# Expert units of a mixture-of-experts block: TensorE's instructions in the order of the program, transposes alternating with the combination, and three more pages for the mixer's weights

## The chip, the core and the metric

The kernel runs on one core of a Trainium2 chip. A core has a matrix engine (TensorE, PE in the profile), a vector engine (VectorE, DVE), an engine for activations (ScalarE, ACT), GpSimd (POOL), and SyncE (SP), which here issues the loads. Matmuls write PSUM banks of 512 floats a partition; the other engines read these. The metric is the device time of one launch in microseconds, the median of several.

## The reference

A decoder block over T = 512 tokens of width 1024, one layer, all in float32: a mixer (a Mamba-2 state-space branch and a gated short convolution on one input projection), then a mixture of experts. The expert part is what the change is about:

```python
scores = sigmoid(hf @ router_w); biased = scores + router_bias
...                                # the best 4 of 8 groups, in them the best 8 of 64 experts
gate = scores[e_idx] / sum * 2.5
...                                # tokens sorted by expert, in blocks
yb = (silu(xb @ w_gate[e]) * (xb @ w_up[e])) @ w_down[e]
routed = segment_sum(yb * row_gate[:, None], row_tok)
```

`w_gate` and `w_up` are 1024 x 256 for each of the 64 experts, `w_down` 256 x 1024: 3 x 64 matrices of 1 MB, 201 MB that are read once. Which tokens an expert gets is known only at run time.

## The kernel before

**Stages.** 0 to 540 us: the modulation (`w_ada`), the layer norm, the input projection and the mixer. 540 to 903: the mixer's output projections, the shared expert, the router and the ranking of the experts by their number of tokens. 903 to 943: the first gathers. 943 to 1605: the routed experts. 1605 to 1640: what is beyond the planned capacities, and the last norm.

**Expert units.** After the ranking, every rank has a fixed capacity in tokens (320, 192, 160, 128, 96, 64, 32). Ranks are packed into blocks of 128 token rows, and blocks into 32 units, whose kinds stand in a string (`ORDER`, one letter a unit): one expert of 128 rows; two experts at 64; four at 32; 96 + 32; and units of a full block and a packed one (three blocks in one unit). There are 41 blocks. A block's tokens are gathered from DRAM by an indirect DMA (L1075, GpSimd), whose indices come from matmuls with one-hot tiles (L1067), reductions (L1070) and an integer tile (L1072); `need_s` starts this. `xsplit`, called by `need_x`, turns the gathered rows with eight transposes (L141) and copies them out of PSUM into `xt` (L878, ScalarE).

**A unit's work** is the generator `ffn` (L905 is the matmul in `tiled`). Four quarters of the contraction come first, two k-steps of 128 each, for gate and up weights together (512 columns). A *full* block (one expert) has a float32 product made of three matmuls of split operands (`matmul3`, L144 to L146; the high part `wh` comes from ScalarE, L149, the low part `wl` from VectorE, L151). A *packed* block is done by `tiled`: one matmul for each expert, each in its own column strip of the array (`tile_position`), so that a k-step is two strips of 64 or four of 32 columns, which work beside each other. In the trace such a float32 matmul is two records. 336 k-steps of this kind are in the units. Behind the fourth quarter `act_t` makes the gate (Silu L886 on ScalarE, product L887 on VectorE), transposes it (L141) and copies it into `wkr` (L896 or a split). After a `yield` come the down matmuls (again `tiled` or `matmul3`, into `ps_y`), and `done` scales a block's output by the gate (L1108, VectorE) and splits it; a one-hot tile `oht` (L1104, GpSimd) says which token each row belongs to.

**Combination.** When two blocks are done, `combine()` adds them to the residual: for 4 token tiles and 2 halves, four matmuls `oht` x output (L1131 and L1132, full array, high and low part) into one of the two `ps_y` banks, and an addition on VectorE (L1137).

**What sets the order.** The steps of neighbouring units are interleaved in the program (quarters 1 to 3 of a unit, quarter 0 of the next, down matmuls of the first). Then a scheduler orders the instructions of every engine by priority and readiness in its own model; it may set any ready instruction between the strips of a k-step. Weight pieces of 1 MB are issued by SyncE, eight pieces ahead (`AHEAD`), into seven page pairs (`pair`, 1 MB, or two pages of 512 KB by `page`) and two more pages. In the mixer every 512 KB weight load (`load_cols`, L174; `ya_load`, L607) takes one of the fourteen pages of that ring. `beyond()` (L1307 to L1329) computes from the counts whether any tokens are left over.

Of the kernel before, what the change touches and what calls it, by code (L numbers as in the profile page):

```python
# [25 lines left out]
NPAIR = 7  # L26
NPAGB = 5
NPAPB = 2
STAT = ((0, 1),)
NST = sum(len(u) for u in STAT)  # L30

CAPS = ((1, 320), (4, 192), (3, 160), (4, 128), (16, 96), (13, 64), (21, 32)) + tuple((len(u), 128 // len(u)) for u in STAT)
GRP = 2
XA = 3
NXG = 3


# [2 lines left out]
NDEF = 2  # L40
FORD = "q0 r0 s0 q1 r1 s1 q2 r2 s2 q3 r3 s3"
NADA = 3
BEY = 100
ENG3 = ("PP", "VV", "VV", "VV")
NWK = 5
AD = "VVVV"
# [15 lines left out]
def block_kernel(ctx: ExitStack, tc: tile.TileContext, a, out, dbg=None):  # L62
# [40 lines left out]
    def page(shape, dt=F32, pool=None):  # L103

        n = 1
        for q in shape:
            n *= q
        assert n == 1024
        if pool:
            return pool.tile([P, *shape], dt, name="pg", tag="pg")  # L110
        assert dt == F32
        if not halves:
            halves.extend(reversed(two([1024])))
        h = halves.pop()
        return h.rearrange("p (a b) -> p a b", a=shape[0]) if len(shape) == 2 else h

    def wk():
        return wkp.tile([P, T], F32, name="wk")

# [50 lines left out]

    def load_cols(w, c0):

        v = page([KD, P])
        SY.dma_start(v, w[:, c0:c0 + P].rearrange("(k p) n -> p k n", p=P))  # L174
        return v

# [426 lines left out]

    def ya_load(qt, j):
        def f():
            v = page([4, 256])
            SY.dma_start(v, a["w_ssd_out"][0, qt * 512:(qt + 1) * 512, j * P:j * P + 256]  # L607
                         .rearrange("(k p) n -> p k n", p=P))
            return v
        plan(("ya", qt, j), f)  # L610
# [112 lines left out]
    for n, _ in enumerate(core):  # L723
        next(sc_g)
        for it in late:
            next(it, None)
    work_cm.__exit__(None, None, None)
    rt = ctx.enter_context(tc.tile_pool(name="rt", bufs=1))
    pb_ = ctx.enter_context(tc.tile_pool(name="pageb", bufs=NPAGB))
    ada4, ada8 = ada_rows(4), ada_rows(8)  # L730
# [132 lines left out]
            SY.dma_start(r, wd.rearrange("(p k) n -> p k n", k=2))  # L863
        return r

    def xsplit(src_ap, dst=None, whole=False):

        hi, lo = dst or [None if whole and i else hold.tile([P, KD, P], F32 if whole else FR, name="xt", tag="hm", bufs=8)
                         for i in range(2)]
        sv = src_ap.rearrange("p (d k) -> p k d", k=KD)  # L870
        for q in range(2):
            tp = bank("tr", 2)
            for k in range(4):
                transpose(tp[:, k * P:(k + 1) * P], sv[:, 4 * q + k, :])
            tv = tp.rearrange("p (k n) -> p k n", k=4)
            sl_ = slice(4 * q, 4 * q + 4)
            if whole:
                S.activation(hi[:, sl_, :], tv, AF.Copy)  # L878
            else:
                split_to(hi[:, sl_, :], lo[:, sl_, :], tv)  # L880
        return hi, lo

    def act_t(o, whole):

        sg = rt.tile([P, FE], F32, name="sg", bufs=2)
        S.activation(sg, o[:, :FE], AF.Silu)  # L886
        V.tensor_tensor(sg, sg, o[:, FE:], op=OP.mult)  # L887
        tp = bank("tr", 2)
        av = sg.rearrange("p (f j) -> p j f", j=2)
        for j in range(2):  # L890
            transpose(tp[:, j * P:(j + 1) * P], av[:, j, :])
        aw = wkp.tile([P, 4, P], F32 if whole else FR, name="wkr", tag="wk")
        ah, al = aw[:, 0:2], aw[:, 2:4]
# [14 lines left out]
    def ffn(blocks, xs, w, done, gp=False):  # L908


        es = sorted({e for b in blocks for e in b})
        split_e = sorted({b[0] for b in blocks if len(b) == 1})
        os_ = [bank(*(("pj", 3) if i < 3 else ("y", 2))) for i in range(len(xs))]
        for q in range(4):
            if q % 2 == 0:
                us = {e: w(e, q // 2) for e in es}
            uq = {e: us[e][:, :, q % 2 * 2:q % 2 * 2 + 2, :] for e in es}
            hl_ = {e: split(uq[e], GP if gp else None) for e in split_e}
            for o, (xh, xl), b in zip(os_, xs, blocks):
                for k in (2 * q, 2 * q + 1):  # L920
                    if len(b) == 1:
                        wh, wl = hl_[b[0]]
                        matmul3(o, xh[:, k, :], xl[:, k, :], wh[:, :, k % 2, :], wl[:, :, k % 2, :], k == 0, k == KD - 1)
                    else:
                        tiled(o, xh[:, k, :], [uq[e][:, :, k % 2, :] for e in b], k == 0, k == KD - 1)
            if q == 3:
                acts = [act_t(o, len(b) > 1) for o, b in zip(os_, blocks)]
            yield
        us = {e: w(e, 2) for e in es}
        wdn = {e: [split(us[e][:, j], GP if gp else None) for j in range(2)] for e in split_e}  # L930
        for i, ((ah, al), b) in enumerate(zip(acts, blocks)):
# [158 lines left out]
    def expert(blocks, sl_, xs, w):  # L1090
# [3 lines left out]
        def done(b, n, o):  # L1094
# [17 lines left out]
                S.activation(rt.tile([P, 1], F32, name="warm"), rw(yh)[:, 0:1], AF.Sqrt, bias=epsc, scale=0.0)  # L1112
            if n == 1:
                parts.append(res_[b])
                if len(parts) == GRP and not tail[0]:
                    combine()

        return ffn(blocks, xs, w, done)

    parts = []  # L1120
    rsum = rt.tile([P, NT, 2], F32, name="rsum")

    def combine(last=False):

        for t in range(NT):
            for n in range(2):
                ns_ = slice(n * 512, (n + 1) * 512)
                o = bank("y", 2)
                for i, (oht, yh, yl) in enumerate(parts):
                    oh_ = oht[:, t * P:(t + 1) * P]  # L1130
                    PE.matmul(o, oh_, yh[:, ns_], start=(i == 0), stop=False)  # L1131
                    PE.matmul(o, oh_, yl[:, ns_], start=False, stop=(i == len(parts) - 1))  # L1132
# [154 lines left out]
        while len(sl) < min(n, len(allb)):  # L1287
            sl.append(allb[len(sl)][1]())

    def need_x(n):  # L1290
        while len(xs) < min(n, len(allb)):
            i = len(xs)
            need_s(i + 1)
            xs.append(xsplit(sl[i][0], None, len(allb[i][0]) > 1))
            need_s(i + NXG)

    iota_t = rt.tile([P, T], F32, name="iota_t", tag="pt")
    GP.iota(iota_t, pattern=[[1, T]], base=0, channel_multiplier=0, allow_small_or_imprecise_dtypes=True)
    def beyond():
# [33 lines left out]
    running, i1 = {}, 0  # L1333
    for i, (u, j) in enumerate(steps):
        if j == 0:
            i0 = ublk[id(u)]
            i1 = i0 + len(u[1])
            need_x(i1)
            running[id(u)] = expert([b for b, _ in u[1]], sl[i0:i1], xs[i0:i1],
                                    lambda e, q, n=unum[id(u)]: take((n, e, q), AHEAD))  # L1340
        if i + XA < len(steps) and steps[i + XA][1] == 0 and len(xs) == i1:
            need_x(i1 + 1)
        if i == BEY:
            ostart, oend, obase, nov = beyond()
        tail[0] = i == len(steps) - 1
        next(running[id(u)], None)
    combine(True)


    ocur = rt.tile([P, 1], F32, name="ocur")  # L1350
# [98 lines left out]
```

## Time and profile before

| | |
|---|---|
| median of 3 runs | 1646.18 us |
| lowest, highest | 1641.13, 1926.16 us |
| profiled execution | 1641.05 us, of it 1639.3 us from the first to the last instruction |
| TensorE busy in the span | 1550.5 us (95%), mean granted clock 0.98 |
| VectorE, ScalarE, GpSimd busy | 988.3, 643.7, 305.0 us |
| DMA | 335.66 MB, mean 205 GB/s |

The records of matmuls overlap: the end of one is modelled and lies behind the start of the next. So a busy share near 100% says that TensorE was never without work, not that each matmul took its recorded time; what a matmul costs is read from its start to the next one's start.

### The profile page before, as it was taken

How to read it: one execution, taken by the hardware profiler on the slowest of the kernel's cores; microseconds unless marked ns; L12 is line 12 of the kernel's file. 1: busy time of each engine (PE TensorE's matmuls, PEld its weight loads, DVE VectorE, ACT ScalarE, POOL GpSimd, SP SyncE). 2: the span in 40 equal slices, each digit the busy share in tenths (PEclk: the TensorE clock that was granted, in tenths of full speed). 3: DMA queues.
4: the chain of work that ended last, by engine and by line, in shares of the span. 5: the costliest groups of instructions: out<-in, count | busy, mean ns of one | idle time of the engine just before them, and what ended most of it. 6: DMA issues, size and time to landing. Idle time of an engine off the chain costs nothing.

```text
span 1639.3 us, 22871 instructions
## 1 busy us (share of the span) xinstructions
PE 1550.5 (95%) x8253; PEld 1011.6 (62%) x8253; DVE 988.3 (60%) x1760; ACT 643.7 (39%) x926; POOL 305.0 (19%) x314
## 2 busy tenths in 40 slices
PE   6999999999999989899988899999999999999996
PEld 3687777777777867688766354554454444446533
DVE  5557778668848757445796363654455455457546
ACT  3556576545634445433552222232222223223323
POOL 0011110111001446500024211111111221112111
PEclk9999999999999989999988999999999999999998
DMA  9654332633450467535553779786978696799771
GB/s 275 170 151 107 82 87 65 153 85 87 116 125 1 155 200 230 164 88 167 199 174 103 253 288 364 273 314 231 369 287 301 249 402 238 280 381 351 277 287 61
DMA packets 193783, 335.66 MB, mean 205 GB/s; under 512 B 13348, under 2 KB 136580, under 8 KB 185348
## 3 DMA queue, kind: packets, MB, share of 16 engines
q1 hardware_dynamic: 182580, 303.73, 54.9%
q0 software_dynamic: 11088, 30.45, 6.8%
q8 instruction: 66, 1.08, 0.3%
q14 instruction: 49, 0.40, 0.1%
HBM read 334.58 MB, written 4.28 MB: 207 GB/s over the span
## 4 chain that ended last, share of the span: by engine, by line
PE 54%; DVE 6%; DMA 5%; POOL 2%; issue 2%; ACT 2%; SPq 0%; ACTq 0%; DVEq 0%; POOLq 0%
PE ps_pj L905 13%; PE ps_y L905 7%; PE ps_pj L144 6%; PE ps_pj L145 5%; PE ps_pj L146 5%; PE ps_y L1131 5%; PE ps_y L1132 5%; PE ps_tr L141 3%; DMA pr<-in_w_ada_dram 3%; POOL pg L357 2%; PE ps_y L144 1%; DVE wl L151 1%; DMA pr<-in_w_up_dram 1%; PE ps_y L145 1%; PE ps_y L146 1%
## 5 line engine op out<-in xcount | busy, mean ns | idle before, releaser
L151 DVE TENSOR_TENSOR wl<-pr,wh 128x1024 fp32r<-128x1024 f32 (+1 forms) x201 | 256.2, 1285 | 153.9 <-ACT wh L149 150.9
L144 PE MATMUL ps_pj<-hm,wh 128*128 128x512 f32 x680 | 276.6, 408 | 9.2 <-ACT wh L149 7.9
L149 ACT ACTIVATE wh<-pr 128x1024 fp32r<-128x1024 f32 (+1 forms) x207 | 201.1, 987 | 192.8 <-PE ps_pj L145 87.9
L146 PE MATMUL ps_pj<-hm,wl 128*128 128x512 f32 x680 | 269.2, 397 | 5.2 <-DVE wl L151 5.2
L145 PE MATMUL ps_pj<-hm,wh 128*128 128x512 f32 x680 | 268.4, 395 | 0.0
L905 PE MATMUL ps_pj<-pr,xt 128*32 128x512 f32 (+1 forms) x1472 | 252.1, 601 | 0.0
L144 PEld LDWEIGHTS ps_pj<-hm,wh 128*128 128x128 f32 x680 | 129.3, 190 | 43.7 <-ACT wh L149 9.9
L146 PEld LDWEIGHTS ps_pj<-hm,wl 128*128 128x128 f32 x680 | 129.1, 190 | 37.0 <-DVE wl L151 8.9
L145 PEld LDWEIGHTS ps_pj<-hm,wh 128*128 128x128 f32 x680 | 129.3, 190 | 29.5 <-issue 3.6
L1108 DVE SCALAR_TENSOR_TENSOR wk<-ps_y,red,pg 128x512 f32<-128x512 f32 x82 | 61.0, 749 | 118.8 <-PE ps_y L905 92.8
L1137 DVE TENSOR_TENSOR res<-res,ps_y 128x512 f32<-128x512 f32 x152 | 103.3, 687 | 47.5 <-PE ps_y L1132 47.0
L905 PEld LDWEIGHTS ps_pj<-pr,xt 128*32 128x32 f32 (+1 forms) x1472 | 58.2, 115 | 119.3 <-issue 114.0
L905 PE MATMUL ps_y<-pr,wkr 128*32 128x512 f32 (+1 forms) x736 | 117.5, 597 | 0.0
L1075 POOL DMA_INDIRECT pg<-h_d,idx x41 | 44.2, 1078 | 349.5 <-PE ps_tr L141 103.8
L1104 POOL TENSOR_SCALAR oht<-iota_t,tok 128x512 fp32r<-128x512 f32 x41 | 70.3, 1721 | 156.2 <-PE ps_y L1132 156.0
L886 ACT ACTIVATE sg<-ps_pj 128x256 f32<-128x256 f32 x44 | 16.9, 384 | 198.0 <-PE ps_pj L905 126.8
L357 POOL TENSOR_TENSOR pg<-pg,pr 128x1024 f32<-128x1024 f32 x28 | 75.3, 2706 | 68.7 <-ACT pr L355 68.6
L144 PE MATMUL ps_pj<-pr,wh 128*128 128x512 f32 x192 | 76.3, 398 | 10.1 <-ACT zs L422 10.1
L145 PE MATMUL ps_pj<-pr,wh 128*128 128x512 f32 x192 | 75.7, 394 | 0.0
L146 PE MATMUL ps_pj<-pr,wl 128*128 128x512 f32 x192 | 75.7, 394 | 0.0
L887 DVE TENSOR_TENSOR sg<-sg,ps_pj 128x256 f32<-128x256 f32 x44 | 18.5, 419 | 90.6 <-ACT sg L886 90.6
L407 DVE SCALAR_TENSOR_TENSOR wk<-ps_pj,cw,wk 128x511 f32<-128x511 f32 (+2 forms) x93 | 68.5, 743 | 7.6 <-ACT wk L405 7.3
(388 smaller groups left out, 2610.3 us busy)
## 6 DMA issues: line engine op xcount, KB each, us to landing
pr<-in_w_gate_dram SPq DMA_DIRECT2D x128, 512.0 KB, 8.3
pr<-in_w_up_dram SPq DMA_DIRECT2D x128, 512.0 KB, 9.0
pr<-in_w_down_dram SPq DMA_DIRECT2D x64, 1024.0 KB, 8.4
pr<-in_w_in_dram SPq DMA_DIRECT2D x88, 512.0 KB, 6.2
pr<-in_w_ada_dram SPq DMA_DIRECT2D x48, 512.0 KB, 5.1
bc<-acs_d POOLq DMA_DIRECT2D x32, 256.0 KB, 5.2
pr<-in_w_ssd_out_dram SPq DMA_DIRECT2D x16, 512.0 KB, 6.6
pr<-in_w_sc_out_dram SPq DMA_DIRECT2D x8, 512.0 KB, 4.8
```

Of the source, the lines that this page charges most:

```text
L144: PE.matmul(o, lh, rh, start=start, stop=False)
L145: PE.matmul(o, lh, rl, start=False, stop=False)
L146: PE.matmul(o, ll, rh, start=False, stop=stop)
L149: S.activation(hi, src, AF.Copy)
L151: V.tensor_tensor(lo, src, rw(hi), op=OP.subtract)
L357: GP.tensor_tensor(part[i], part[i], w, op=OP.add)
L407: V.scalar_tensor_tensor(acc[:, s:], o[:, :T - s], cw[:, 3 - s, tl:tl + 1], acc[:, s:], op0=OP.mult, op1=OP.add)
L905: PE.matmul(o[w * i:w * i + w, :], x[:, w * i:w * i + w], m, start=start, stop=stop, tile_position=(0, w * i))
L1104: GP.tensor_scalar(res_[b][0], iota_t, tok, None, op0=OP.is_equal)
L1131: PE.matmul(o, oh_, yh[:, ns_], start=(i == 0), stop=False)
L1132: PE.matmul(o, oh_, yl[:, ns_], start=False, stop=(i == len(parts) - 1))
L1137: V.tensor_tensor(ra[t][:, ns_], ra[t][:, ns_], o, op=OP.add)
```

## The change

It has two parts.

*The expert units.* `xsplit` and `combine` become generators, `xsteps` and `csteps`; the former yields after four transposes, the latter after the four matmuls and the addition of a bank. `act_t` is cut in two: `act_in` (Silu and product), and `act_t` (transposes), with a `yield` before and one behind it. A new `unit(n)` writes the order out: quarters 1 to 3 of unit n, quarter 0 of unit n+1 (`begin`), the transposes of n's activations, then the token transposes of unit n+2 alternating with a combination if two blocks are done (or the ring of outputs would be full), then n's down matmuls. In odd quarters the blocks of a unit come in reverse. From the third unit on this stands in `tc.manual_schedule(engines={PE})`: TensorE's instructions keep the order of the program, while the other engines are ordered by the scheduler as before. `beyond()` moves from the 100th step of the old list to just ahead of the unit with number 25.

*The mixer's loads.* `wpage` hands out, in turn, one of three new pages `sp` of the working pool and a page of the old ring, until the working pool is closed ahead of the experts.

```diff
+NSTR = 3
-XA = 3
+NRING = 3
+MAN = 2
-BEY = 100
+BEY = 25
...
+    def wpage(shape):
+
+        strm[0] += 1
+        if strm[0] % 2 and strm[0] > 0:
+            return work.tile([P, *shape], F32, name="sp", tag="sp", bufs=NSTR)
+        return page(shape)
...
     def load_cols(w, c0):
 
-        v = page([KD, P])
+        v = wpage([KD, P])
...
     def ya_load(qt, j):
         def f():
-            v = page([4, 256])
+            v = wpage([4, 256])
...
     work_cm.__exit__(None, None, None)
+    strm[0] = -1 << 30
...
-    def xsplit(src_ap, dst=None, whole=False):
+    def xsteps(src_ap, dst=None, whole=False):
...
+        def steps():
+            for q in range(2):
+                tp = bank("tr", 2)
+                for k in range(4):
+                    transpose(tp[:, k * P:(k + 1) * P], sv[:, 4 * q + k, :])
...
+                yield
+
+        return (hi, lo), steps()
...
-    def act_t(o, whole):
+    def act_in(o):
 
         sg = rt.tile([P, FE], F32, name="sg", bufs=2)
         S.activation(sg, o[:, :FE], AF.Silu)
         V.tensor_tensor(sg, sg, o[:, FE:], op=OP.mult)
+        return sg
+
+    def act_t(sg, whole):
+
         tp = bank("tr", 2)
...
-            for o, (xh, xl), b in zip(os_, xs, blocks):
+            for o, (xh, xl), b in list(zip(os_, xs, blocks))[::-1 if q % 2 else 1]:
...
             if q == 3:
-                acts = [act_t(o, len(b) > 1) for o, b in zip(os_, blocks)]
+                sgs = [act_in(o) for o in os_]
             yield
+        acts = [act_t(sg, len(b) > 1) for sg, b in zip(sgs, blocks)]
+        yield
...
                 parts.append(res_[b])
-                if len(parts) == GRP and not tail[0]:
-                    combine()
...
-    def combine(last=False):
-
+    def csteps(last=False):
+
+        ps_ = list(parts)
+        parts.clear()
         for t in range(NT):
             for n in range(2):
...
                     V.tensor_tensor(ra[t][:, ns_], ra[t][:, ns_], o, op=OP.add)
-        parts.clear()
+                yield
...
+    def begin(n):
+
+        u = units[n]
+        i0 = ublk[id(u)]
+        i1 = i0 + len(u[1])
+        need_x(i1)
+        running.append(expert([b for b, _ in u[1]], sl[i0:i1], xs[i0:i1], lambda e, q: take((n, e, q), AHEAD)))
+        next(running[n])
+
+    def unit(n):
...
+        u, last = units[n], n + 1 == len(units)
+        for _ in range(3):
+            next(running[n])
+        if not last:
+            begin(n + 1)
+        next(running[n])
+        xg_ = xs_steps(ublk[id(units[n + 2])] + len(units[n + 2][1])) if n + 2 < len(units) else iter(())
+        if len(parts) >= GRP or len(parts) + len(u[1]) > NRING or last and parts:
+            zipper(xg_, csteps())
+        else:
+            drain(xg_)
+        tail[0] = last
+        next(running[n], None)
...
+    with tc.manual_schedule(engines={mybir.EngineType.PE}):
+        for n in range(MAN, len(units)):
+            if n == BEY:
+                ostart, oend, obase, nov = beyond()
+            unit(n)
+        combine(True)
```

TensorE, in the second half of the units, a unit of four 32-column strips, before. One row of the order is one matmul instruction (two records in the trace); `ps_pj` is the gate and up product, `ps_y` a down product or a combination, `ps_st` the index matmul.

```order
L1067 MATMUL ps_st<-pay,oh 128x6
L905 MATMUL ps_pj<-pr,xt 32x512
L1131 MATMUL ps_y<-hm_70,oht 128x512
L1132 MATMUL ps_y<-hm_71,oht 128x512
L1131 MATMUL ps_y<-pr,oht 128x512
L1132 MATMUL ps_y<-pr,oht 128x512
...
L905 MATMUL ps_pj<-pr,xt 32x512 x28
L141 MATMUL ps_tr<-ident,sg 128x128 x2
L905 MATMUL ps_pj<-pr,xt 32x512 x3
L141 MATMUL ps_tr<-ident,pg 128x128 x4
L905 MATMUL ps_y<-pr,wkr 32x512 x16
```

The first strip of a k-step stands ahead of twenty combination matmuls, the other three behind them. The same engine after, a unit of that kind at the turn from one unit to the next:

```order
L931 MATMUL ps_pj<-pr,xt 32x512 x8
L152 MATMUL ps_tr<-ident,sg 128x128 x2
L152 MATMUL ps_tr<-ident,pg 128x128 x4
L1160 MATMUL ps_y<-pr,oht 128x512
L1161 MATMUL ps_y<-pr,oht 128x512
L1160 MATMUL ps_y<-rww,oht 128x512
L1161 MATMUL ps_y<-pg,oht 128x512
L152 MATMUL ps_tr<-ident,pg 128x128 x4
...
L931 MATMUL ps_y<-pr,wkr 32x512 x16
```

Quarter 0 of the next unit (x8) is whole, then come the gate's two transposes, then four token transposes and four combination matmuls in turn. In the order of the whole expert part, 77 of the 336 packed k-steps are cut by other instructions before, and 10 after, all of these in the first two units; TensorE changes from packed to full-array matmuls 130 times before and 65 times after.

ScalarE, after, at a turn from a unit to one with a full expert; `wh` is the high part of a weight piece, `sg` the Silu of the gate.

```order
L892 ACTIVATE xt<-ps_tr 128x512 x2
L160 ACTIVATE wh_80<-pr 128x1024
L160 ACTIVATE wh_76<-pr 128x1024
L160 ACTIVATE rww<-wk 128x512 x2
L160 ACTIVATE wh_78<-pr 128x1024
L160 ACTIVATE wh_80<-pr 128x1024
L908 ACTIVATE sg<-ps_pj 128x256
```

Two weight splits stand directly ahead of a Silu; ScalarE was ordered in this manner before as well.

SyncE, after, the first loads:

```order
L185 DMA sp<-in_w_ada_dram 128x8x128
L185 DMA pr<-in_w_ada_dram 128x8x128
L185 DMA sp<-in_w_ada_dram 128x8x128
L185 DMA pr<-in_w_ada_dram 128x8x128
L242 DMA wdt<-in_w_in_dram 128x8x32
L185 DMA sp<-in_w_in_dram 128x8x128
L185 DMA pr<-in_w_in_dram 128x8x128
```

Before, the same loads all went to `pr`; now every second one takes one of the three `sp` pages, in the same order.

## Rows read from the trace of the kernel before

**Rows 1.** Busy time by stage: stretch, length, engines, granted clock, DMA share, GB/s.

```profile
core 0: us, PE busy (x) PEld busy (x) DVE busy (x) ACT busy (x) POOL busy (x), PEclk, DMA share, GB/s
0.00:540.00 540.00, 507.90 (x2638) 395.27 (x2639) 374.20 (x720) 286.61 (x381) 57.91 (x120) 0.99 0.47 116
...
943.00:1605.00 662.00, 653.58 (x3804) 324.33 (x3803) 349.72 (x579) 182.21 (x293) 111.20 (x109) 1.00 0.82 303
```

**Rows 2.** Waits of TensorE, 943 to 1605: total us, times, longest.

```profile
PE ps_pj L145 <- DVE wl L151: 2.5, 3, 0.9
PE ps_pj L144 <- ACT wh L149: 1.7, 2, 1.6
```

**Rows 3.** TensorE's timeline, 1286 to 1312: start, busy us, instructions.

```profile
1292.89 1.05 PE L905 MATMUL ps_pj<-pr,xt 128*32 128x512 f32 x2
1293.87 0.50 PE L1131 MATMUL ps_y<-hm,oht 128*128 128x512 f32 x1
1294.20 0.39 PE L1132 MATMUL ps_y<-hm,oht 128*128 128x512 f32 x1
1294.43 0.39 PE L1131 MATMUL ps_y<-pr,oht 128*128 128x512 f32 x1
...
1298.61 0.40 PE L1132 MATMUL ps_y<-pr,oht 128*128 128x512 f32 x1
1298.93 6.21 PE L905 MATMUL ps_pj<-pr,xt 128*32 128x512 f32 x56
...
1307.32 3.64 PE L905 MATMUL ps_y<-pr,wkr 128*32 128x512 f32 x32
1310.90 0.71 PE L141 MATMUL ps_tr<-ident,pg 128*128 128x128 f32 x4
```

**Rows 4.** Groups of TensorE's instructions, 943 to 1605: busy us, mean ns, idle before.

```profile
L905 PE MATMUL ps_pj<-pr,xt 128*32 128x512 f32 (+1 forms) x1360 | 231.0, 599 | 0.0
L905 PE MATMUL ps_y<-pr,wkr 128*32 128x512 f32 (+1 forms) x656 | 106.6, 597 | 0.0
```

**Rows 5.** Costliest groups of the page, whole span, same columns.

```profile
L151 DVE TENSOR_TENSOR wl<-pr,wh 128x1024 fp32r<-128x1024 f32 (+1 forms) x201 | 256.2, 1285 | 153.9 <-ACT wh L149 150.9
...
L149 ACT ACTIVATE wh<-pr 128x1024 fp32r<-128x1024 f32 (+1 forms) x207 | 201.1, 987 | 192.8 <-PE ps_pj L145 87.9
...
L1137 DVE TENSOR_TENSOR res<-res,ps_y 128x512 f32<-128x512 f32 x152 | 103.3, 687 | 47.5 <-PE ps_y L1132 47.0
...
L886 ACT ACTIVATE sg<-ps_pj 128x256 f32<-128x256 f32 x44 | 16.9, 384 | 198.0 <-PE ps_pj L905 126.8
...
L887 DVE TENSOR_TENSOR sg<-sg,ps_pj 128x256 f32<-128x256 f32 x44 | 18.5, 419 | 90.6 <-ACT sg L886 90.6
```

**Rows 6.** Groups of VectorE's instructions in `beyond()`, 1380 to 1390.

```profile
L1309 DVE TENSOR_TENSOR key<-ps_st,caprow 128x64 f32<-128x64 f32 x1 | 0.2, 224 | 4.2 <-PE ps_st L1307 4.2
...
L1313 DVE SCALAR_TENSOR_TENSOR rem<-key,rem 128x64 f32<-128x64 f32 x3 | 0.7, 226 | 0.1
```

**Rows 7.** Busy time in slices of 41 us of the expert stretch.

```profile
984.00:1025.00 41.00, 37.52 (x221) 17.64 (x213) 14.56 (x32) 9.95 (x16) 6.67 (x8) 1.00 0.96 366
...
1107.00:1148.00 41.00, 40.93 (x175) 19.59 (x176) 19.16 (x30) 9.89 (x17) 7.83 (x9) 1.00 0.63 233
...
1476.00:1517.00 41.00, 40.86 (x237) 25.30 (x236) 29.58 (x39) 14.48 (x22) 10.67 (x10) 1.00 0.92 350
```

**Rows 8.** DMA issues (KB each, us to landing), and ScalarE's wait for one.

```profile
pr<-in_w_gate_dram SPq DMA_DIRECT2D x128, 512.0 KB, 8.3
pr<-in_w_up_dram SPq DMA_DIRECT2D x128, 512.0 KB, 9.0
...
ACT wh L149 <- DMA pr<-in_w_up_dram: 19.5, 4, 11.7
```

**Rows 9.** Waits of SyncE's queue and TensorE, 0 to 540, and the DMA share at the start.

```profile
SPq L607 <- DVE wl L151: 158.8, 9, 39.8
SPq L174 <- DVE wl L151: 154.1, 11, 22.3
...
PE ps_pj L144 <- ACT zs L422: 10.1, 5, 3.6
...
6.00:48.00 42.00, 34.64 (x295) 21.84 (x296) 21.04 (x43) 13.06 (x22) 0.00 (x0) 1.00 1.08 279
```

More of the change, by code (lines that the diff above doesn't have):

```diff
@@ L115, in page @@
         return h.rearrange("p (a b) -> p a b", a=shape[0]) if len(shape) == 2 else h
+    strm = [0]
+    def wpage(shape):
[3 more added lines that the diff above has]
+        return page(shape)
     def wk():
@@ L870, in xsplit @@
         sv = src_ap.rearrange("p (d k) -> p k d", k=KD)
[L871 to L881, printed above, removed]
-    def act_t(o, whole):
+        def steps():
[3 more added lines that the diff above has]
+                    transpose(tp[:, k * P:(k + 1) * P], sv[:, 4 * q + k, :])
+                tv = tp.rearrange("p (k n) -> p k n", k=4)
+                sl_ = slice(4 * q, 4 * q + 4)
+                if whole:
+                    S.activation(hi[:, sl_, :], tv, AF.Copy)
+                else:
+                    split_to(hi[:, sl_, :], lo[:, sl_, :], tv)
+                yield
+        return (hi, lo), steps()
+    def xsplit(src_ap, dst=None, whole=False):
+        r, g = xsteps(src_ap, dst, whole)
+        for _ in g:
+            pass
+        return r
+    def act_in(o):
         sg = rt.tile([P, FE], F32, name="sg", bufs=2)
@@ L1128, in combine @@
                 o = bank("y", 2)
-                for i, (oht, yh, yl) in enumerate(parts):
+                for i, (oht, yh, yl) in enumerate(ps_):
                     oh_ = oht[:, t * P:(t + 1) * P]
                     PE.matmul(o, oh_, yh[:, ns_], start=(i == 0), stop=False)
-                    PE.matmul(o, oh_, yl[:, ns_], start=False, stop=(i == len(parts) - 1))
+                    PE.matmul(o, oh_, yl[:, ns_], start=False, stop=(i == len(ps_) - 1))
                 if last:
@@ L1137, in combine @@
                     V.tensor_tensor(ra[t][:, ns_], ra[t][:, ns_], o, op=OP.add)
-        parts.clear()
+                yield
+    def combine(last=False):
+        for _ in csteps(last):
+            pass
     out_proj(0)
@@ L1288, in need_s, with xs_steps @@
             sl.append(allb[len(sl)][1]())
-    def need_x(n):
+    def xs_steps(n):
         while len(xs) < min(n, len(allb)):
@@ L1293, in need_x @@
             need_s(i + 1)
-            xs.append(xsplit(sl[i][0], None, len(allb[i][0]) > 1))
+            r, g = xsteps(sl[i][0], None, len(allb[i][0]) > 1)
+            xs.append(r)
+            yield from g
             need_s(i + NXG)
+    def need_x(n):
+        drain(xs_steps(n))
     iota_t = rt.tile([P, T], F32, name="iota_t", tag="pt")
@@ L1330, in beyond @@
         return ostart, oend, obase, nov
-    need_x(1)
[L1333 to L1347, printed above, removed]
+    running = []
+    def begin(n):
[15 more added lines that the diff above has]
+            zipper(xg_, csteps())
+        else:
+            drain(xg_)
+        tail[0] = last
+        next(running[n], None)
+    need_x(1)
+    begin(0)
+    need_x(ublk[id(units[1])] + len(units[1][1]))
+    for n in range(MAN):
+        unit(n)
[3 more added lines that the diff above has]
+                ostart, oend, obase, nov = beyond()
+            unit(n)
+        combine(True)
     ocur = rt.tile([P, 1], F32, name="ocur")
```

## The prediction

> **What bounds the kernel now.** I read the busy time of each stage first. The expert stretch, 943 to 1605 us, is 662 us of the 1639.3, and TensorE is recorded busy in 653.58 of them at a granted clock of 1.00; VectorE is busy 349.72 and ScalarE 182.21 [rows 1]. The waits of TensorE there say the same: the two largest are 2.5 us in three and 1.7 us in two [rows 2]. So the stretch is TensorE's, and nothing is gained by making its operands come earlier.
>
> The next view is TensorE's own timeline, read from start to start, since the records overlap. Full 128-column matmuls follow each other every 0.23 us (1294.20, 1294.43). Tiled matmuls work beside each other in column strips: four whole k-steps of a unit of four 32-column strips, 32 records, take from 1307.32 to 1310.90, 3.58 us, so 0.87 us a k-step (with the change-over to the transposes in it). But at 1292.89 two records of one strip stand alone, because the scheduler put twenty combination matmuls after the first strip of a k-step. They hold the engine until 1293.87: 0.98 us for a quarter of a k-step [rows 3]. A piece of a k-step costs as much as a whole one, and the busy view calls it busy. That is where this change can gain anything: tiled matmuls are the largest group of the stretch, 231.0 + 106.6 us of busy time [rows 4].
>
> **The change, part by part.** *Whole tiled k-steps.* I counted the k-steps in the built order of both kernels. In the part of the 32 units there are 336; before, 77 of them are broken in 83 places, and TensorE goes through 394 stretches of a k-step's price instead of 343 after (some pieces of two blocks run beside each other, so 83 breaks cost fewer). After, 10 are broken, all in the first two units, which the scheduler still orders. 51 stretches fewer at 0.86 us (0.87 less its share of the change-over): **-44 us**. All of it lies on the path, as TensorE is the path.
>
> *Changes between tiled and full.* The order has 130 changes from tiled to full before and 65 after. One round trip costs: 0.11 (0.98 against 0.87 in the last tiled stretch), 0.10 (1293.87 to 1294.20 is 0.33 against 0.23) and 0.09 (1298.61 to 1298.93 is 0.32 against 0.23) [rows 3], together 0.30. 65 x 0.30: **-19.5 us**. The combination, transposes and full matmuls are as many as before and keep their prices.
>
> *Waits that the fixed order adds.* A scheduler's order fills TensorE with whatever is ready; a program order can't. In each of the 30 units from the third on, two things have to be back in time. First, the gate: Silu on ScalarE (0.384) and the product on VectorE (0.419) [rows 5], with the hand-overs between them about 1.0 us, an estimate. Its cover is quarter 0 of the next unit, two tiled k-steps, 1.72 us. It is late only if an operation is running ahead of it: the longest frequent ones are 1.285 us on VectorE (the low part of a weight split) and 0.987 on ScalarE (the high part) [rows 5]. With both in the way it takes 3.27 us, and 1.55 are left uncovered. VectorE is busy 53% and ScalarE 28% of the stretch [rows 1], so half such an operation is met half the time on the one and a quarter of the time on the other, about 0.5 us: 1.5 in all, just under the cover. Second, the transposed activations must be copied out before the down matmuls; where a combination stands between, it covers that, and about half of the units have only the next tokens' transposes. Behind a TensorE that waits for either, everything of the unit waits; nothing passes it. Bounds: 0, and 30 x (1.55 + 1.0) = 76 us. I take 0.4 us a unit, near the low end, because the mean case is covered: **+12 us**.
>
> *Combination alternating with transposes.* Four combination matmuls fill a bank in 0.92 us, and VectorE's addition that frees it is 0.687 [rows 5]. With two banks even a weight split (1.285) ahead of an addition makes 1.97 against 1.84. I cost it at nothing; VectorE covers it at 53% busy, and if that cover went, 0.13 us for each such meeting.
>
> *The counts of overflow.* `beyond()` moves behind the 25th unit and into the fixed order. It has about seven small VectorE steps near 0.226 us [rows 6], with two small matmuls and a transpose among them; before, VectorE waited 4.2 us within it and TensorE did other work. Now TensorE stands for the chain once: **+2.2 us**, between 0 and 6.
>
> *The weight stream.* The same 201 MB of experts must come in a shorter stretch. Of the sixteen slices of 41 us, five have a DMA share of 0.92 or more, the first at 984 (0.96), the last at 1476 (0.92), while the one at 1107 has 0.63 [rows 7]. The saving spread evenly is 63.5 x 41 / 662 = 3.9 us a slice; where the engines are already full a slice can't shrink, unless the slice ahead of it loads more. The pages that let it do so are as many as before. Bounds 0 and 5 x 3.9 = 19.7 us; I take two slices of five, because the eight pieces on hand are 8 MB, 26 us at the stretch's 303 GB/s [rows 1], so that a part of each full slice can come in the one before: **+7.5 us**.
>
> *Mixer loads over three more pages.* SyncE waits 158.8 + 154.1 us for pages, which look like a limit; but TensorE's largest wait there, 10.1 us, is for an activation of ScalarE, not for a weight [rows 9]. More pages let loads go earlier and nobody is waiting for them: 0 gained, at most 3. There is a cost at the start. From 6 to 48 us the DMA share is 1.08 [rows 9]: the loads themselves are the limit, and now every other load has to wait for one of only three pages, where all took their turn over the fourteen of the ring. Bound +5; I take **0** for both, as the engines, not the pages, are full there.
>
> Sum against the profiled execution: 1641.1 - 44 - 19.5 + 12 + 2.2 + 7.5 = **1599 us**. The median of the three runs is 1646.18, 5 us above the profiled one, so a measured median may lie some us higher too. 2% of the median, about what a measurement of this kernel tells from no change, is 33 us.
>
> **The rivals.**
> *A: the new waits eat the saving.* If in every unit the gate comes behind a split on both engines, 30 x 1.55 = 46 us replace my 12: 1633 us, no change. For it: the scheduler still orders VectorE and ScalarE, and has put two splits right ahead of a Silu, as the order shows. Against it: 53% busy. The Trainium skill, "TensorEngine Tiling (Array Packing)", section "PSUM Bottleneck", says that after tiling has made TensorE faster the copies out of PSUM may become the bottleneck; by that rule this rival is likelier than I make it. That VectorE has 312 free microseconds in the stretch speaks against the rule here. Chance 0.19.
>
> *B: busy is busy.* If TensorE's 653.58 us were all needed, at most the 8.4 idle ones can be won: 1633. The lone strip's 0.98 us speaks against it. The Trainium skill, "Trainium Kernel Development and Optimization", section "Performance Expectations", calls matmul busy time a bad metric because matmuls are pipelined; the trace agrees (two records of 0.39 start 0.23 apart). Chance 0.06.
>
> *C: slower, through ScalarE's queue.* ScalarE's order puts the next unit's weight splits, which wait for a DMA, ahead of this unit's Silu. Before, TensorE went on with something else, so ScalarE's 19.5 us of waiting in four such places (the longest 11.7) [rows 8] cost little. In the fixed order TensorE waits with it. There are 12 units with a full expert; if each one loses a landing of about 8.7 us less the cover of 1.7, that is 84 us: 1683. It beats the saving from 42 / 12 = 3.5 us a unit on, and is slower by 2% from about 6.5. Against it: loads run eight pieces ahead, and only four such waits were seen. Chance 0.11.
>
> *D: the stream decides.* All five full slices keep their length: 19.7 in place of 7.5, 1611 us. Chance 0.14.
>
> That the change does not keep the k-steps whole is excluded by the order itself.
>
> **How the numbers follow.** My forecast has the other 0.50, with 1576 (no new waits, no loss to the stream, mixer 3 better) to 1613 as its own range. Faster by over 2% (below 1613): forecast and D, 0.64. Within 2%: A and B, 0.25. Slower: C, 0.11. The range runs from 1576 to 1640, so that A, B and D with up to 5 us of a slower start are inside, and C is outside with some of the forecast's lower end.
>
> **What the changed profile would show.** Whole k-steps: no tiled row of two records between combination rows, and the tiled groups' busy sum down from 337.6. The length from the first expert unit to the tail, 662 now, near 620. New waits: rows of TensorE's transposes waiting for the product of L909, about 12 us in all; 40 or more mean A, and waits of ScalarE's splits for DMA followed by TensorE's for Silu mean C. D shows as slices at a share of 1.0 with TensorE waiting for splits that wait for DMA. At the start, the stretch of 6 to 48 us longer by more than 3 us means that three pages are too few. I am wrong if the stretch shrinks by less than 25 us with fewer than 30 us of waits in it: then a piece of a k-step doesn't cost what I read from it.

## The result, and the profile after

The changed kernel takes 1706.75 us (median of four, 1702.42 to 1712.1), against 1645.32 before: ratio 1.038 [1.034, 1.043]. It is slower by 61 us, where 1599 had been forecast. The ratio leaves out one run of the kernel before, which at 1926.16 us fell into a slower state than all others. The profiled execution has a span of 1707.1 us. The same stages as in [rows 1], with their columns:

```profile
0.00:540.00 540.00, 509.80 (x2635) 395.44 (x2636) 370.40 (x719) 282.37 (x378) 59.85 (x120) 0.98 0.46 116
...
940.00:1667.00 727.00, 642.64 (x3810) 325.68 (x3806) 340.64 (x563) 184.87 (x295) 109.44 (x107) 0.95 0.75 277
```

The part ahead of the experts is no longer than it was: the first block's output is scaled at 926.0 us, before at 926.4. The expert stretch has grown from 662 to 727 us, although TensorE is busy *less* in it: 642.6 against 653.6. So it stood still for longer, and its granted clock fell from 1.00 to 0.95. What it waited for there, the answer to [rows 2]:

```profile
PE ps_pj L931 <- DMA pr<-in_w_up_dram: 27.1, 16, 5.1
PE ps_pj L155 <- ACT wh L160: 12.8, 7, 4.6
PE ps_tr L152 <- DVE wkr L162: 5.6, 5, 3.0
PE ps_tr L152 <- ACT wkr L922: 5.3, 7, 2.2
PE ps_pj L156 <- DVE wl L162: 5.0, 7, 0.8
PE ps_tr L152 <- DMA pg<-h_d,idx: 4.7, 1, 4.7
PE ps_y L931 <- DMA pr<-in_w_down_dram: 4.5, 5, 1.5
```

Weights come first (27.1, and the splits behind them). The chain of the gate, from the Silu to the copy into `wkr`, comes to some 15 us (5.6 and 5.3 for the copies, 3.8 for the product), near the 12 of the prediction. TensorE's timeline shows both costs of a late weight, and what the change did gain (compare [rows 3]):

```profile
949.50 0.49 PE L155 MATMUL ps_pj<-wh,xt 128*128 128x512 f32 x1 [1.33 <-ACT wh L160]
950.76 0.80 PE L156 MATMUL ps_pj<-wl,xt 128*128 128x512 f32 x1 [0.77 <-DVE wl L162]
951.36 0.63 PE L157 MATMUL ps_pj<-wh,xt 128*128 128x512 f32 x1
951.78 0.63 PE L155 MATMUL ps_pj<-wh,xt 128*128 128x512 f32 x1
952.21 0.63 PE L156 MATMUL ps_pj<-wl,xt 128*128 128x512 f32 x1
...
984.00 3.64 PE L931 MATMUL ps_y<-pr,wkr 128*32 128x512 f32 x32
987.46 1.90 PE L931 MATMUL ps_pj<-pr,xt 128*32 128x512 f32 x16
994.12 1.46 PE L931 MATMUL ps_pj<-pr,xt 128*32 128x512 f32 x2 [4.76 <-DMA pr<-in_w_up_dram]
```

Tiled matmuls now stand in whole k-steps: four from 984.00 to 987.46, 0.87 us each. But behind the pauses at 949.50 and 950.76 a full matmul starts every 0.43 us (951.78, 952.21) instead of 0.23, which is the lower of the clock's two levels, 1.2 in place of 2.4 GHz: the pause is paid a second time. And at 994.12 even a tiled k-step stops for a piece of weights. SyncE's own queue says why that piece was late:

```profile
946.95 0.34 SPq L872 DMA_DIRECT2D pr<-in_w_up_dram  x1
947.99 11.10 SPq L875 DMA_DIRECT2D pr<-in_w_down_dram  x2
987.75 0.34 SPq L872 DMA_DIRECT2D pr<-in_w_gate_dram  x1
```

Between the two down pieces at 948 to 959 and 987.75 no weight is issued. In this hole SyncE waits first for a page that a split on VectorE is reading, then for one that a down product is reading:

```profile
SPq L872 <- PE ps_y L931: 14.8, 1, 14.8
SPq L872 <- DVE wl L162: 13.5, 1, 13.5
```

In the whole expert stretch the waits for down products are the largest of SyncE's, with 249.5 us at the gate and up loads, and 12.2 at the down loads; before, the two were 22.3 and 109.1.

```profile
SPq L872 <- PE ps_y L931: 249.5, 23, 19.8
```

The second page comes free with the down products at 984.00 to 987.46, which the fixed order puts behind a combination and a gather. In slices of 20 us (compare [rows 7]) the engines' share falls and rises:

```profile
940.00:960.00 20.00, 17.91 (x95) 6.57 (x90) 5.16 (x6) 3.15 (x4) 0.00 (x0) 0.83 0.91 357
960.00:980.00 20.00, 14.73 (x103) 10.50 (x102) 11.63 (x24) 6.69 (x12) 2.27 (x2) 0.91 0.22 78
980.00:1000.00 20.00, 12.18 (x69) 4.37 (x67) 7.13 (x12) 2.52 (x4) 4.92 (x5) 0.87 0.63 200
1000.00:1020.00 20.00, 16.13 (x67) 6.79 (x66) 3.47 (x4) 3.85 (x6) 0.00 (x0) 0.79 0.97 391
```

The DMA engines idle at 0.22 first and are full at 0.97 when it is too late. That the stream as a whole were too slow (rival D) does not fit this: its mean share is 0.75, less than before (0.82).

### The profile page after: what moved, and what is told of

The parts are those of the page before. It is cut to its first block, busy times and chain, and to the rows that moved or that the text cites. A ratio compares the mean times of both kernels' runs of the same rounds, so it can differ in the third digit from the quotient of the medians.

```text
span 1707.1 us, 22880 instructions
## 1 busy us (share of the span) xinstructions
PE 1543.8 (90%) x8253; PEld 1013.4 (59%) x8253; DVE 975.4 (57%) x1752; ACT 641.9 (38%) x924; POOL 307.5 (18%) x314
## 4 chain that ended last, share of the span: by engine, by line
PE 43%; DMA 13%; DVE 9%; ACT 3%; issue 2%; POOL 1%; SPq 1%; ACTq 0%; DVEq 0%; POOLq 0%
PE ps_pj L931 8%; PE ps_y L931 6%; DMA pr<-in_w_up_dram 5%; PE ps_pj L156 5%; PE ps_pj L155 5%; PE ps_pj L157 5%; PE ps_y L1160 4%; PE ps_y L1161 4%; DMA pr<-in_w_down_dram 3%; PE ps_tr L152 3%; DVE wl L162 3%; DMA pr<-in_w_ada_dram 2%; POOL pg L368 1%; ACT wh L160 1%; PE ps_y L155 1%
## 5 line engine op out<-in xcount | busy, mean ns | idle before, releaser
L162 DVE TENSOR_TENSOR wl<-pr,wh 128x1024 fp32r<-128x1024 f32 (+1 forms) x154 | 195.8, 1278 | 168.4 <-ACT wh L160 167.9
L931 PE MATMUL ps_pj<-pr,xt 128*32 128x512 f32 (+1 forms) x1472 | 243.3, 624 | 29.5 <-DMA pr<-in_w_up_dram 27.1
L160 ACT ACTIVATE wh<-pr 128x1024 fp32r<-128x1024 f32 (+1 forms) x160 | 162.1, 1026 | 154.0 <-PE ps_pj L156 41.6
L931 PEld LDWEIGHTS ps_pj<-pr,xt 128*32 128x32 f32 (+1 forms) x1472 | 62.0, 119 | 180.9 <-issue 153.8
L1166 DVE TENSOR_TENSOR res<-res,ps_y 128x512 f32<-128x512 f32 x144 | 98.3, 686 | 85.6 <-PE ps_y L1161 84.5
L931 PE MATMUL ps_y<-pr,wkr 128*32 128x512 f32 (+1 forms) x736 | 111.6, 606 | 5.2 <-DMA pr<-in_w_down_dram 4.5
L152 PE MATMUL ps_tr<-ident,pg 128*128 128x128 f32 x360 | 59.6, 293 | 24.3 <-DMA pg<-h_d,idx 10.6
L160 ACT ACTIVATE hm<-wk 128x512 fp32r<-128x512 f32 (+1 forms) x66 | 28.7, 468 | 133.7 <-DVE wk L1137 99.9
```

What stands on the lines that cost most here:

```text
L152: return PE.transpose(o, i, ident[:n, :n])
L160: S.activation(hi, src, AF.Copy)
L162: V.tensor_tensor(lo, src, rw(hi), op=OP.subtract)
L931: PE.matmul(o[w * i:w * i + w, :], x[:, w * i:w * i + w], m, start=start, stop=stop, tile_position=(0, w * i))
```

## The experiments

The kernel before was run beside each; its median was 1637.6 to 1641.1 us in the four groups of runs. Where I compare stretches, I take them from the scaling of the first block's output to that of the last (41 blocks), so that the mixer is left out.

### The two halves of the change

**mixer_only**: the kernel before with `NSTR`, `wpage` and its two uses. 

> The kernel before with the three sp pages alone. The trace after reaches the router 5.1 us earlier than the one before (876.1 against 871.0 us), so if that came from the pages the whole kernel takes 1640 us, ratio 0.997. If the mixer's gain was chance or came from the scheduler's other choices, 1645, ratio 1.000.

Measured: 1679.6 us, ratio 1.024 [1.022, 1.027]. This was a surprise: the "harmless" half alone costs 42 us.

**units_only**: the changed kernel with both uses of `wpage` turned back, this one and the one in `ya_load`.

```diff
-        v = wpage([KD, P])
+        v = page([KD, P])
```

> The change without the sp pages: the fixed order of the expert units alone. All of the loss should be here: 1707 + 5 = 1712 us, ratio 1.040. If the pages of the mixer had a part in the loss, below 1700.

Measured: 1650.6 us, ratio 1.007 [1.005, 1.009]. So the first part of the change alone costs some 12 us and not 61. The stretches, first of the kernel before, then of mixer_only and of units_only:

```profile
926.40:1611.10 684.70, 675.64 (x3984) 334.24 (x3984) 362.25 (x601) 193.51 (x311) 114.08 (x112) 1.00 0.81 300
```

```profile
924.40:1647.90 723.50, 707.52 (x3972) 337.92 (x3972) 363.50 (x602) 193.04 (x310) 116.12 (x112) 1.00 0.77 285
```

```profile
930.90:1621.60 690.70, 640.45 (x3966) 333.91 (x3966) 355.17 (x585) 192.81 (x307) 113.91 (x110) 0.97 0.80 298
```

With the sp pages alone the loss lies in the *experts*, where no sp page exists: 723.5 us against 684.7 before, and it is TensorE's busy time that grew, by 32 us. Without them the fixed order is busy for 640.5 only.

### How pages of the mixer can slow the experts

`page` cuts a pair of 1 MB into two halves and keeps the second half in a list for the next call. `wpage` takes away 45 of these calls, an odd number; I counted the list while the kernels were built: one half is left when the experts begin, none before. The last norm's `ln2g = page([D])` uses it, so its pair stays taken through all experts: six pairs in place of seven.

**after_even** and **mixer_even**: the changed kernel, and mixer_only, with the half given up.

```diff
+    halves.clear()
     shw = [piece(q, a["sh_gate"][0], a["sh_up"][0], a["sh_down"][0]) for q in range(3)]
```

> The changed kernel with one line more: the half of a page pair that is left over when the mixer is done is given up ahead of the experts. Counted while the program is built, one half is left over after the change and none before; it is next used by the last norm, so its pair (1 MB of the seven) would be held through all experts. Theory 1, the lost pair makes the weights late: the loss of the sp pages goes and their gain in the mixer stays, 1650.6 - 4 = 1646 us, ratio about 1.005. Theory 2, the sp pages hurt in another way (the mixer's scheduling, where the pools lie): 1700 us or more.

> The sp pages alone, with the left-over half given up ahead of the experts. Theory 1: what is left is the mixer's gain, 3 to 5 us: 1635 us, ratio 0.997. Theory 2: still 1675 to 1680.

Measured: after_even 1637.7 us, ratio 0.998 [0.995, 1.000]; mixer_even 1635.7, ratio 0.997 [0.995, 0.998]. One line takes 69 us from the changed kernel, and 44 from the sp pages alone.

**before_odd**: `page([D])` on a line of its own at the same place of the kernel before. 

> The kernel before with one page taken ahead of the experts and not used, so that one half is left over and a pair is held to the end; no sp pages, no fixed order. Theory 1: the loss of the run with the sp pages alone comes back without them, 1639 + 40 = 1679 us, ratio 1.024. Theory 2: 1639 us, ratio 1.000.

Measured: 1639.6 us, ratio 1.000 [0.997, 1.002]. This miss was the experiment's: nothing touches that pair until the last norm, so it can have been held only then; TensorE's order was that of before, row for row.

**before_held**: the same page, written once, so that it is really held.

```diff
+    GP.memset(page([D]), 0.0)
     shw = [piece(q, a["sh_gate"][0], a["sh_up"][0], a["sh_down"][0]) for q in range(3)]
```

> As the run before_odd, but the page that is taken ahead of the experts is also written once by GpSimd, so that its pair is really in use from there to the last norm (in before_odd nothing touched it until the last norm, and TensorE's order was that of the kernel before). No sp pages, no fixed order, one small operation more. Theory 1, the held pair alone makes the loss of the run with the sp pages: 1678 us, ratio 1.024. Theory 2, something else of the sp pages does: 1640 us.

Measured: 1685.2 us, ratio 1.027 [1.025, 1.030]. A held pair alone, with no other part of the change, makes the loss. Its stretch, and that of mixer_even:

```profile
929.40:1654.70 725.30, 708.58 (x3972) 339.11 (x3972) 363.36 (x601) 192.79 (x310) 115.82 (x112) 1.00 0.77 284
```

```profile
916.70:1601.30 684.60, 676.41 (x3984) 335.02 (x3984) 362.09 (x601) 193.37 (x311) 113.16 (x112) 1.00 0.81 300
```

Under the scheduler the lost pair shows as busy time (708.6 against 676.4), because it changes the order that the scheduler makes. The traces show this directly. From the first unit on, TensorE's records stand in the same order, row for row, in before_held and in mixer_only, and again in mixer_even and in the kernel before. Between these two orders the stretches of tiled matmuls (each ended by any other matmul) rise from 148 to 170, and those of them that begin or end inside a k-step from 100 to 131.

In the fixed order TensorE's records hardly change (99 of 4150 stand differently in the changed kernel and in after_even), and the lost pair shows as waits and as lower clock. The stretch of the changed kernel, to be set beside that of after_even below:

```profile
926.00:1679.70 753.70, 669.25 (x3966) 338.74 (x3966) 354.87 (x586) 192.88 (x308) 112.64 (x110) 0.95 0.74 273
```

So the pair is worth 41 us of the stretch under the scheduler, and 64 in the fixed order. Of the 64, 37 are idle time and 27 busy time; the lower clock accounts for some 9 of these 27, an estimate, and the rest was not taken apart.

### What is left of the fixed order

With the pair back, the fixed order is 2 us slower than the scheduler's by the medians (after_even against mixer_even), hardly more than the noise, where 42 us of gain had been forecast. In the profiled executions the stretches differ by 5.3 us. That of after_even:

```profile
922.20:1612.10 689.90, 642.18 (x3966) 336.26 (x3966) 355.30 (x585) 192.65 (x307) 113.11 (x110) 0.97 0.80 298
```

TensorE is busy for 642.2 us against 676.4 in mixer_even, it is idle for 47.7 against 8.2, and its clock is 0.97 against 1.00. In two parts, the first ten units (15 blocks) and all that follow, this is after_even, then man10_even (below), then mixer_even:

```profile
922.20:1211.20 289.00, 257.72 (x1414) 134.44 (x1414) 137.43 (x226) 73.01 (x117) 45.40 (x44) 0.94 0.76 285
1211.20:1612.20 401.00, 384.56 (x2560) 201.82 (x2556) 217.93 (x361) 119.75 (x190) 67.71 (x67) 0.99 0.82 307
```

```profile
920.00:1185.30 265.30, 262.46 (x1414) 129.12 (x1414) 136.73 (x227) 72.31 (x117) 44.79 (x44) 1.00 0.83 311
1185.30:1585.70 400.40, 384.14 (x2560) 201.36 (x2556) 218.07 (x361) 119.97 (x190) 67.62 (x67) 0.99 0.82 307
```

```profile
916.70:1182.10 265.40, 260.67 (x1462) 129.98 (x1459) 138.81 (x240) 73.29 (x119) 44.84 (x47) 1.00 0.83 309
1182.10:1601.30 419.20, 415.74 (x2527) 205.04 (x2525) 223.28 (x361) 120.08 (x192) 68.32 (x65) 1.00 0.80 295
```

So the fixed order gains 18 us behind the first ten units, and loses 24 us in them.

**man10_even**: after_even with `MAN = 10`. 

> The changed kernel with the left-over half given up, with TensorE in the fixed order from the 11th unit on only; the first ten units, in which four units of four experts and the unit of three blocks stand, are left to the scheduler. If the fixed order loses in these units by late weights, whose stalls the scheduler fills with other work, and gains behind them: from block 10 to block 40 the fixed order won 13 us against the kernel before, so 1636 - 13 = 1623 us. If the loss comes at every place where the fixed order begins (first gathers, first weights): 1640.

Measured: 1618.2 us, ratio 0.987 [0.984, 0.989]. The later units take 401 and 400 us in the fixed order (after_even, man10_even) and 419 in the scheduler's; the first ten cost the fixed order 289 us, and the scheduler 265. (Among them are two units of four experts, not four as the expectation says, and they end with the 15th block, not with the tenth.)

**no_down_even**, **no_down_after**, **no_down_before**: a third of the stream left out, in after_even, the changed kernel and the kernel before (`AHEAD = 12` in all three; `DownW` stands for a vector tile in SBUF).

```diff
     def expert_piece(sel_, q):
 
+        if q == 2:
+            return DownW()
```

> The changed kernel with the left-over half given up and without the loads of the down weights (a third of the experts' bytes is left out; page lead 12 pieces, that is 8 loads). In the full kernel with the half given up TensorE waited 18.8 us for DMAs in the expert stretch, nearly all in the first ten units, and its clock was at 0.79 to 0.91 there. If those units are short of weights, the loss of 25 us by the tenth block goes: 1637.7 - 30 = 1608 us. If they wait for the first gathers and for the chain behind them, whatever the weights: 1630 us.

> The changed kernel without the loads of the down weights (every expert's down product reads one vector tile that is already in SBUF; the page lead in pieces goes from 8 to 12, which is again 8 loads): a third of the experts' bytes is left out. Theory 1, the weights come late because pages are held too long or the stream is too slow: the waits for weights in the expert stretch (27.1 + 12.8 + 5.0 + 4.5 + 2.1 us) and most of what the lower clock costs go, some 80 us: 1625 us. Theory 2, the fixed order loses its time in the chain from Silu to the down products, whatever the loads do: 1690 to 1705 us.

> The kernel before without the loads of the down weights, in the same manner. TensorE waited 7.2 us in the whole expert stretch, so by the trace the loads cost it nothing: 1635 to 1645 us. If the scheduler's order hid late weights behind other work, still the same. Under 1620 would mean that the stream had set the length of the stretch before as well.

Measured: 1622.0, 1628.8 and 1623.9 us (ratios 0.988 [0.985, 0.991], 0.993 [0.991, 0.996] and 0.991 [0.989, 0.993]). The changed kernel gains 78 us, the kernel before 14, after_even 16. The 64 us between the first two are about the whole loss of the changed kernel, so late weights make it. Once the pair is back, fewer bytes are worth hardly more to the fixed order than to the scheduler's: 16 us against 14. The expectations for no_down_even (30 or 8 us) and no_down_before (no gain, or over 17) were both missed, between their two values. In the first ten units of the traces the difference is larger: they take 266 us in no_down_even against 289 in after_even, and 253 in no_down_before against 266 in the kernel before. By these traces about 10 of the 24 us that the fixed order loses there go with late weights, an estimate; what makes the rest was not separated. The waits of after_even up to 1123 us, then of no_down_even:

```profile
PE ps_pj L931 <- DMA pr<-in_w_up_dram: 13.6, 6, 3.4
PE ps_tr L152 <- DMA pg<-h_d,idx: 4.5, 1, 4.5
```

```profile
PE ps_pj L155 <- ACT wh L160: 7.8, 2, 4.2
PE ps_tr L152 <- DMA pg<-h_d,idx: 3.5, 1, 3.5
```

The tiled k-steps no longer wait; one gather and the splits remain, and the wait for splits is longer than it was (2.8 us in after_even).

### Other places in the order

**q1_even**: after_even with the combination behind the next unit's quarter 1, so behind the down products. 

```diff
-        for _ in range(3):
+        cg_ = csteps() if len(parts) >= GRP or len(parts) + len(u[1]) > NRING or last and parts else iter(())
+        for m in (8, 0, 0):
             next(running[n])
+            drain(islice(cg_, m))
```

> The changed kernel with the left-over half given up, and with the combination in another place of the fixed order: behind the next unit's quarter 1, thus after the down products of the unit that completes it, instead of ahead of the down products, alternating with the token transposes. If pages are held too long because the combination stands ahead of the down products (whose pages SyncE waits for), the stalls of the first 160 us of the expert stretch go: 1615 us. If the first units are short of weights in any fixed order, the same as with the combination ahead, 1646 us. If the missing cover between Silu and down products costs more, above 1655.

Measured: 1632.9 us, ratio 0.996 [0.994, 0.998], 5 us better than after_even; 1615 had been expected. TensorE's waits for weights fell from 14.4 to 2.5 us in the whole stretch, and in the profiled executions the first ten units took 269 us where after_even took 289. That fits the reading that the place of the down products decides when the pages come free. But the later units took 408 us instead of 401, and VectorE's additions, now without transposes between them, make TensorE wait:

```profile
PE ps_y L1163 <- DVE res L1169: 7.4, 10, 3.2
PE ps_tr L152 <- ACT wkr L922: 4.6, 8, 0.8
```

**q1_beyond** and **spread_beyond**: q1_even with `beyond()` called ahead of the fixed order; and the same with `(3, 3, 2)`. 

> As q1_even (combination behind the next unit's first quarter, left-over half given up), with the counting of overflow taken out of the fixed order: it is placed ahead of it, where the scheduler can spread its seven steps. In q1_even TensorE waits for it at 1460 to 1500 us (32.7 us busy of 40, granted clock 0.91). That stretch gives 6 to 10 us back: 1625 us. If the waits come back at the start of the fixed order instead: 1632.

> As q1_beyond, with the combination's eight banks spread behind three quarters (3, 3 and 2) instead of all behind one. VectorE then has a quarter's time for its additions (q1_even: TensorE waited 7.4 us for a bank) and the weights are used more evenly, but each unit with a combination has two more round trips between tiled and full matmuls, 16 x 2 x 0.3 = 10 us: 1625 - 7 + 10 = 1628 us. If late weights are still the main loss: 1615.

Measured: 1626.1 us, ratio 0.992 [0.990, 0.994], and 1630.4, ratio 0.994 [0.992, 0.996], both within 3 us of what was expected.

**man10_beyond** and **man10_q1**: man10_even with `beyond()` ahead of the ninth unit; and the same with the combination as in q1_even. 

> As man10_even (1618.2 us), with the counting of overflow moved ahead of the fixed order, among the units that the scheduler orders. In man10_even TensorE waits 3.6 + 1.7 us for it and the clock falls to 0.91 in 1460 to 1500 us. Without these: 1618 - 8 = 1610 us. If the scheduler's units pay for it: 1616.

> As man10_beyond, and the combination behind the next unit's quarter 1 in all units instead of ahead of the down products. With whole lead (no lost pair) from the 11th unit on, TensorE waits little for weights (2.3 us for DMAs in man10_even), so pages that come free earlier gain nothing there, and the combination no longer covers the copy of the gate: 1612 us, no better than man10_beyond. If late weights still decide: 1600.

Measured: 1614.1 us, ratio 0.983 [0.980, 0.985], and 1624.2, ratio 0.989 [0.987, 0.992]. man10_beyond is the fastest of all, 1.7% below the kernel before. man10_q1 is 10 us slower than it, where 2 had been expected: behind the first ten units it takes 401.5 us and man10_beyond 392.1, so where the weights are on hand the later place of the combination costs 9 us, and only where they are short does it gain. The stretch in which `beyond()` had stood, in man10_even and then in man10_beyond:

```profile
1440.00:1500.00 60.00, 53.17 (x344) 28.65 (x348) 40.53 (x71) 21.48 (x31) 11.35 (x11) 0.94 0.79 296
```

```profile
1440.00:1500.00 60.00, 57.74 (x388) 33.86 (x390) 42.66 (x68) 24.24 (x35) 12.35 (x12) 1.00 0.93 355
```

TensorE is busy for 4.6 us more and back at its full clock. The median falls by 4 us.

## Why the prediction was wrong

**The step that failed** is one sentence in *The weight stream*: "The pages that let it do so are as many as before." I had compared the pools, which say so, and not who holds their pages when the experts begin. One pair of seven was held by a left-over half. This is shown in three ways: giving it up takes 69 us from the changed kernel; holding one in the kernel before adds 45, in the very order of mixer_only; and a third fewer bytes takes 78 from the changed kernel and 14 from the kernel before. Accordingly the term for the mixer's loads, taken as 0 with at most 3 us of gain and 5 of loss, was a loss of 42 (mixer_only). What I had reasoned about there came out a little better than forecast: with the pair back the new pages gain 5 us (mixer_even).

With the pair back after_even lies inside the stated range, but 39 us from the forecast; so the other terms have to be looked at too.

**Whole k-steps and fewer changes, -63.5.** The mechanism held. From mixer_even to after_even, which differ in the first part of the change alone, TensorE's busy time fell by 34.2 us, although its clock was lower. By the trace the lower level lasted 44 us of this stretch, and TensorE was busy in 34 of them, which is 17 us of work; in mixer_even it was 2. So the work became some 50 us cheaper, an estimate, with whole k-steps and fewer changes together. One reading was a little off: 3.58 us for four k-steps is 0.895 each, and 0.87 holds without the change-over (3.46 for four in the changed kernel); that is about 1 us of the sum. Rival B (busy is busy) is refuted: TensorE was busy in 99% of the stretch before, and the same products took 34 us less. Here the trace agrees with the Trainium skill ("Trainium Kernel Development and Optimization", section "Performance Expectations") that matmul busy time is a bad metric for how close a kernel is to its roofline.

**New waits, +12.** The chain that I had priced, from the Silu to the down products, was of the right size: it is about 10 us of the waits in after_even. What I had not priced as waits is larger. Idle time rose by 39.5 us (8.2 to 47.7); of the 47.7, weights are 14.4, splits 7.6, one gather 4.5 and `beyond()` 5.6. The lower clock, for which I had no term at all, took some 15 more. The sum -50 + 39.5 + 15 gives the 5 us between the two stretches by construction, and proves nothing.

**`beyond()`, +2.2.** Mis-sized: it waits 3.6 + 1.7 us in the fixed order, and taking it out of there gave 4 and 7 us (man10_beyond, q1_beyond). In man10_even the clock of that stretch was 0.94 and without it 1.00, so a part of this is clock.

**The weight stream, +7.5, and rival D.** The rate of the DMA engines (mean share 0.80 in after_even) was not what fell short, but the release of pages. SyncE's hole is there with seven pairs as well (from 950 to 984.6 us in after_even), and q1_even, which puts the down products ahead of the combination, cuts the waits for weights from 14.4 to 2.5 us with the same bytes. How much of the 24 us lost in the first ten units is late weights stays open; the runs without down weights account for about 10.

**Rival C**, the only slower one, was not it. The splits did make TensorE wait 12.8 us in the changed kernel, but for its full matmuls; for the product behind the Silu, where C had its place, it waited 3.8 us. Rival A was not it either: TensorE's waits for VectorE's products, additions and copies of the gate are some 7 us in after_even, where A needed 46.

## What to carry to other kernels

When a change alters how often a shared pool is asked, look at who holds its pages where the next stage begins: a half of a pair with one late reader costs a whole pair for all that time, and the code of that stage shows nothing. An order that follows the program needs loads that are early enough without filler; where weights are short, write the step that frees a page ahead of the one that doesn't, or leave that stretch to the scheduler and fix the order only behind it. Give the clock a term of its own when you price pauses of the matrix engine: in after_even it cost some 17 us beside 47.7 us of pauses, and in man10_beyond, with 14.2 us of pauses, nothing.

## What the runs showed of the hardware

One strip of a tiled k-step held TensorE for 0.98 us with the change-over behind it, a whole k-step for 0.87; taking the pieces and the changes away made some 50 us of work disappear from 676, an estimate. Where pauses of 0.8 to 5 us came in close succession, the granted clock of the four 20 us slices shown was between 0.79 and 0.91, and full matmuls then started every 0.43 us instead of 0.23. With the scheduler's order in the same units the clock was 1.00 (man10_even). Pauses alone do not settle it: the slice from 1360 to 1380 us of the changed kernel had 3.3 idle us of 20 and kept 1.00. How the two are tied to one another in detail was not tried.
